# Output projections 2 and 3 as one Strassen product of 1024 tokens with operands scaled first; both groups' norms in the FFN

## The chip, the cores and the metric

The kernel runs on one core of one Trainium2 chip. The metric is device time in microseconds (us) of one execution; the number given for a kernel is the median of its runs.

## What is computed

One layer of a decoder trunk, 2048 tokens, width 1024, all in float32. Two groups of heads (a gated recurrence, "hgrn", and stick-breaking attention) each give 512 columns, which are normed per row, joined and sent through one output projection. A feed-forward network and a gated embedding follow. The part that the change touches:

```
o_hg = rmsnorm(hgrn2_mix(hq, hf, hi, lb), hg_out_norm) * silu(hg)
o_sb = rmsnorm(stick_breaking_mix(sq, sk, sv), sb_out_norm)
mix = concat([o_hg, o_sb], -1) @ w_out          # (2048, 1024) @ (1024, 1024)
h = h + rmsnorm(mix, attn_post_norm)
u = rmsnorm(h, ffn_pre_norm)
gate, up = split(u @ w_gate_up)
```

## The kernel before

Tokens are in four groups of 512 (`GT`), and the width is cut into 8 slices of 128 (`ND`; `HH` = 4 is half of it). A product in float32 is three matmuls: each operand is split into a rounded high part (a copy on ScalarE, ACT) and a low part (a subtraction on VectorE, DVE, or on GpSimd, POOL), and `mm3` (L214) adds hi x hi, hi x lo and lo x hi in one PSUM bank.

Stages follow each other: the input projection of the four groups with attention and hgrn woven in; output projections 0 to 3; gate/up, down and the embedding for two token pairs of 1024 each. The attention and hgrn outputs go to DRAM as `o_s[g][0..7]`, transposed, slices 0 to 3 from hgrn and 4 to 7 from attention.

An output projection (`out_proj(g)`, L640) takes the eight slices as operands (`out_load`, L618) and goes through four column quarters of the weights, two halves of the sum each (hgrn, attention), each with matmuls 256 columns wide: 384 a group. The norm of an input row is one factor per token, so it is put on after the matmul: ACT empties the hgrn half with the row's scale (L678), DVE adds the attention half with its own (L680). `post_mix(g)` (L693) norms `mix` (DVE L704), adds `x` (L705, DVE for one half and POOL for the other), norms again (ACT L709) and stores the rows to `un_s[g]` (L710). `turn` (L730) loads them (L737), transposes them on TensorE (L753), four per slice, applies the gain and stores `u_s[g]` (L759). Group 3 is different: its norms run late, in gate/up (`post_late`, L713), from rows stored to `h2_s`.

Gate/up, down and the embedding use Strassen's seven products over 1024 tokens: with both operands as 2 x 2 blocks, seven block products instead of eight, in the order `CHAIN` = 1, 2, 6, 3, 7, 5, 4 (L901), whose sums are chained: `chain` (L929) adds each product from PSUM to a running sum on DVE (L826 is that addition). Their weights' sums are made beforehand (`combos`), their token operands by `t_first` (L863, products 1, 2, 6) and `t_second` (L872, the rest).

The order of TensorE's work is written by hand: `weave(main, slots, ...)` (L51) takes two steps of `main` per slot and between them a share of steps of the other streams. The other engines' instructions are put in order by a scheduler; each engine and SyncE (SP), which issues the DMAs, then runs its own list strictly in order. Around the change the loop was: `post_mix(0)` and `turn(un_s[0])` beside output projection 1; `post_mix(1)` beside projection 2 and 3, `turn(un_s[1])` beside projection 3, together with the operands of gate/up's first three products (`first_operands`, `third_operands`); in gate/up, by hooks at its steps, `t_second`, `post_late(3)`, `turn` of groups 2 and 3.

## Time and profile before

| | us |
|---|---|
| median of 3 runs | 2997.5 |
| least and most of them | 2997.17, 2997.6 |
| the profiled execution's own time | 2997.89 |
| its span | 2995.8 |
| output projections 2 and 3, first to last of their time on TensorE | 1328.5 to 1456.5 |

The profiled execution is the source of all durations. Its engines are PE (TensorE), DVE (VectorE), ACT (ScalarE), POOL (GpSimd) and SP (SyncE). A group's row names the line, the engine, the operation, `out<-in` and its shape, then busy time, mean ns of one, and the idle time of the engine just before with what ended it. A row of waits reads: waiting instruction, releaser, total us, count, longest.

### The profile page before, as it was taken

The numbers are of one execution on the slowest core, as the hardware profiler recorded it, in microseconds if no ns is written. First come the engines' busy times: TensorE is split into PE (matmuls) and PEld (weight loads), VectorE is DVE, ScalarE is ACT, GpSimd is POOL, SyncE is SP. The second block draws the span as 40 slices with busy tenths as digits, with TensorE's granted clock in tenths as the row PEclk, the third lists the DMA queues.
The fourth block names the chain that finished last, engine by engine and source line by source line (L and its number), as shares of the span: only waits on it lengthen the run. The fifth ranks groups of instructions, "written<-read, shape, count | busy, mean of one in ns | idle before, by whom it ended". The sixth has DMA issues, their size and how long they took to land. (4 is left out here: it accounts for less than half of the span.)

```text
span 2995.8 us, 52519 instructions
## 1 busy us (share of the span) xinstructions
PE 2897.3 (97%) x18188; PEld 2425.5 (81%) x18188; DVE 2061.5 (69%) x2993; ACT 1581.0 (53%) x3182; POOL 1405.1 (47%) x1396
## 2 busy tenths in 40 slices
PE   8899999999999999897899999999999999999999
PEld 7788888888887888787788888788788888878777
DVE  3566667687777776755887687665777765656685
ACT  5666756676767676756533333455433323545542
POOL 3344555555556666754532222355622121456653
PEclk9999999999999999999999999999999999999999
DMA  7675665465445544567866787776965555677974
GB/s 215 205 214 166 184 177 165 146 179 166 150 142 152 151 145 128 163 201 244 281 201 197 245 289 253 249 206 213 339 203 163 166 176 176 207 219 230 328 249 162
DMA packets 469417, 602.26 MB, mean 201 GB/s; under 512 B 43168, under 2 KB 277664, under 8 KB 469152
## 3 DMA queue, kind: packets, MB, share of 16 engines
q1 hardware_dynamic: 469152, 598.91, 63.4%
q8 instruction: 144, 2.36, 0.3%
q14 instruction: 121, 0.99, 0.1%
HBM read 439.89 MB, written 158.86 MB: 200 GB/s over the span
## 5 line engine op out<-in xcount | busy, mean ns | idle before, releaser
L818 ACT CAST wh<-wr 128x512 fp32r<-128x512 f32 x600 | 351.6, 618 | 491.7 <-PE z L216 126.5
L819 POOL TENSOR_TENSOR wl<-wr,wh 128x512 fp32r<-128x512 f32 x256 | 371.1, 1456 | 466.2 <-ACT wh L818 426.8
L441 POOL TENSOR_TENSOR a<-be,ring 128x512 f32<-128x512 f32 (+2 forms) x320 | 320.4, 1002 | 411.6 <-DVE ring L437 372.8
L819 DVE TENSOR_TENSOR wl<-wr,wh 128x512 fp32r<-128x512 f32 x344 | 305.2, 895 | 177.5 <-ACT wh L818 160.0
L215 PE MATMUL mm<-uh,wh 128*128 128x512 f32 x992 | 411.3, 415 | 8.1 <-DVE vv L356 3.5
L217 PE MATMUL mm<-uh,wl 128*128 128x512 f32 x992 | 390.8, 394 | 0.0
L216 PE MATMUL mm<-ul,wh 128*128 128x512 f32 x992 | 389.5, 393 | 0.0
L437 DVE TENSOR_TENSOR_SCAN ring<-z,ring,be 128x512 f32<-128x512 f32 x192 | 245.7, 1280 | 101.9 <-ACT z L423 97.3
L215 PE MATMUL mm<-wh,uh 128*128 128x256 f32 (+1 forms) x936 | 287.3, 307 | 4.9 <-DVE vv L356 4.8
L216 PE MATMUL mm<-wl,uh 128*128 128x256 f32 (+1 forms) x936 | 273.5, 292 | 1.1 <-POOL wl L202 1.0
L217 PE MATMUL mm<-wh,ul 128*128 128x256 f32 (+1 forms) x936 | 273.1, 292 | 0.0
L201 ACT CAST wh<-wr 128x512 fp32r<-128x512 f32 x288 | 178.3, 620 | 130.7 <-PE mm L216 69.6
L202 POOL TENSOR_TENSOR wl<-wr,wh 128x512 fp32r<-128x512 f32 x144 | 190.0, 1320 | 103.7 <-ACT wh L201 91.7
L422 ACT ACTIVATE be<-z 128x512 f32<-128x512 f32 (+2 forms) x320 | 171.1, 535 | 106.5 <-DVE z L420 67.8
L215 PEld LDWEIGHTS mm<-uh,wh 128*128 128x128 f32 x992 | 187.6, 189 | 46.8 <-DVE eb L342 3.8
L454 DVE TENSOR_TENSOR al<-tr,ah 128x512 fp32r<-128x512 f32 (+1 forms) x320 | 191.5, 599 | 47.8 <-ACT ah L452 45.8
L217 PEld LDWEIGHTS mm<-uh,wl 128*128 128x128 f32 x992 | 186.9, 188 | 43.2
L819 POOL TENSOR_TENSOR wl<-s,wh 128x512 fp32r<-128x512 f32 x44 | 75.3, 1713 | 305.6 <-ACT wh L818 285.1
L216 PEld LDWEIGHTS mm<-ul,wh 128*128 128x128 f32 x992 | 187.9, 189 | 32.6
L452 ACT CAST ah<-tr 128x512 fp32r<-128x512 f32 (+1 forms) x320 | 167.8, 524 | 79.8 <-PE tr L449 74.6
L215 PEld LDWEIGHTS mm<-wh,uh 128*128 128x128 f32 x936 | 179.7, 192 | 13.4 <-issue 2.6
L416 PE MATMUL z<-kt,q 128*128 128x512 f32 (+3 forms) x640 | 187.8, 375 | 0.0
(312 smaller groups left out, 7559.9 us busy)
## 6 DMA issues: line engine op xcount, KB each, us to landing
wr<-in_w_gate_up_dram SPq DMA_DIRECT2D x308, 256.0 KB, 3.9
wr<-in_w_in_dram SPq DMA_DIRECT2D x224, 256.0 KB, 3.1
wr<-hid_s SPq DMA_DIRECT2D x154, 256.0 KB, 3.3
wr<-in_w_down_dram SPq DMA_DIRECT2D x110, 256.0 KB, 3.5
wr<-wd_s SPq DMA_DIRECT2D x88, 256.0 KB, 3.0
kt<-k_s SPq DMA_DIRECT2D x80, 256.0 KB, 3.3
vt<-v_s SPq DMA_DIRECT2D x80, 256.0 KB, 3.2
wr<-h_s SPq DMA_DIRECT2D x80, 256.0 KB, 4.2
```

The lines of the kernel that those rows point to most:

```text
L201: nc.scalar.copy(hi, src)
L202: (lo_engine or nc.gpsimd).tensor_tensor(lo, src, hi.bitcast(F32), op=ALU.subtract)
L215: nc.tensor.matmul(o, l[0], r[0], start=start, stop=False)
L216: nc.tensor.matmul(o, l[0], r[1], start=False, stop=False)
L217: nc.tensor.matmul(o, l[1], r[0], start=False, stop=stop)
L416: nc.tensor.matmul(z[:, :n], st["q"][i][:, tb * P:(tb + 1) * P], ch["k"][:, :n], start=i == 0, stop=i == 1)
L422: nc.scalar.activation(be[:, :n], z[:, :n], AF.Sigmoid, scale=0.125)
L437: nc.vector.tensor_tensor_scan(r[:, o:o + n][:, ::-1], z[:, :n][:, ::-1], be[:, :n][:, ::-1], init, op0=ALU.mult, op1=ALU.bypass)
L441: nc.gpsimd.tensor_tensor(a[:, :n], be[:, :n], r[:, o + 1:o + n + 1], op=ALU.mult)
L454: nc.vector.tensor_tensor(lo[:, lo_c:], tr[:, lo_c:], hi[:, lo_c:].bitcast(F32), op=ALU.subtract)
L818: nc.scalar.copy(hi, src)
L819: lo_engine.tensor_tensor(lo, src, hi.bitcast(F32), op=ALU.subtract)
```

## The change

Output projections 2 and 3 become one product of 1024 tokens, `out_pair(2)`. Its left operand is [group 2; group 3] x [hgrn half, attention half], its right one is `w_out` in four blocks; the seven products each take four row tiles x four slices x three matmuls of 512 columns.

Since Strassen adds blocks of the operands, the row factors can't be put on afterwards. So the operands are scaled first: `over_rows` turns a row factor into a tile that has it along every partition (a broadcast transposed on PE, copied by ACT), `scaled` multiplies (and applies the attention gain) and stores to `on_s`. For group 2 this is `first_rows(2)`, beside output projection 1, where group 3's squares of slices 4 to 6 are summed too. Group 3's own slices are loaded at the head of `out_pair`, and their scales are made at steps (0,1), (0,3) and (1,1) of it (product's place in the chain, row tile).

The sums of the weight blocks are made by `out_combos` in the first input projection (16 loads, 16 DVE subtractions, 16 stores to `wo_s`). `post_mix(1)`, `turn(un_s[1])` and `first_operands` are woven into `out_pair`; product 6's operands of gate/up move into gate/up's hooks, where its first two blocks now run products 1, 2 of each before 6 of each. The norms of group 2 are done late, as group 3's were (`post_late(2)`). Attention's rest is spread over 30 slots instead of 32.

Three places of the order. First SP, around the last attention tile's store (`avo` to `o_s[3][7]`). Before:

```order
L605 DMA o_s_3_140<-gate 128x512
L623 DMA raw<-o_s_3_140 128x512
L623 DMA raw<-o_s_4_141 128x512
L623 DMA raw<-o_s_5_142 128x512
L623 DMA raw<-o_s_6_143 128x512
L759 DMA u_s_99<-ev 128x512
L210 DMA wr<-in_w_out_dram 128x2x256
L472 DMA o_s_7_144<-avo 64x512
L210 DMA wr<-in_w_out_dram 128x2x256
L623 DMA raw<-o_s_7_144 128x512
```

And in the changed kernel, where L964 is a load to a `wr` tile and L474 the same store:

```order
L920 DMA u_s_99<-ev 128x512
L866 DMA h_s_88<-h 128x512
L474 DMA o_s_7_152<-avo 64x512
L866 DMA h_s_88<-h 128x512
L964 DMA wr<-o_s_0_145 128x512
L964 DMA wr<-o_s_1_146 128x512
L964 DMA wr<-o_s_2_147 128x512
L964 DMA wr<-o_s_3_148 128x512
L964 DMA wr<-o_s_4_149 128x512
L964 DMA wr<-o_s_5_150 128x512
L964 DMA wr<-o_s_6_151 128x512
L964 DMA wr<-o_s_7_152 128x512
```

All eight loads of group 3 stand behind that store, where four stood ahead of it and one behind. Second PE, around the first transposes of `un_s[1]`. Before, in output projection 3:

```order
L215 MATMUL z<-wh,uh 128x256
L216 MATMUL z<-wl,uh 128x256
L217 MATMUL z<-wh,ul 128x256
L753 MATMUL tr<-ident,xt 128x128 x4
L215 MATMUL mm<-wh,uh 128x256
L216 MATMUL mm<-wl,uh 128x256
L217 MATMUL mm<-wh,ul 128x256
```

Now, where the matmuls on bank `z` are the last of product 3's second row tile, those on `av` the first of its third, and L914 is the transposes:

```order
L217 MATMUL z<-wh,uh 128x512
L218 MATMUL z<-wl,uh 128x512
L219 MATMUL z<-wh,ul 128x512
L914 MATMUL tr<-ident,wr 128x128 x4
L217 MATMUL av<-wh,uh 128x512
L218 MATMUL av<-wl,uh 128x512
L219 MATMUL av<-wh,ul 128x512
```

The transposes have moved to between these two row tiles. Third DVE, around the last two row tiles of `post_mix(1)` (the L704 that reads `rstd`). Before:

```order
L704 SCALAR_TENSOR_TENSOR mix<-mix,rstd_18309,gb 128x512 x2
L819 TENSOR_TENSOR ul<-wr,uh 128x512
L705 TENSOR_TENSOR h<-h,mix 128x512
L202 TENSOR_TENSOR wl<-wr,wh 128x512
L819 TENSOR_TENSOR ul<-wr,uh 128x512 x4
L680 SCALAR_TENSOR_TENSOR mix<-z,rg,mix 128x256
L704 SCALAR_TENSOR_TENSOR mix<-mix,rstd_18403,gb 128x512 x2
L819 TENSOR_TENSOR wl<-wr,wh 128x512
L705 TENSOR_TENSOR h<-h,mix 128x512
```

Now L864 and L865 are those lines, L987 reading a bank is the chain addition, L204, L774 and L980 are splits; `c_18794`, `c_18839` and `c_18900` belong to product 3's row tiles 0, 1 and 2:

```order
L987 TENSOR_TENSOR c_18794<-mm,cu 128x512
L204 TENSOR_TENSOR ul<-wr,uh 128x512
L774 TENSOR_TENSOR ul<-wr,uh 128x512
L987 TENSOR_TENSOR c_18839<-z,cu 128x512
L204 TENSOR_TENSOR ul<-wr,uh 128x512
L864 SCALAR_TENSOR_TENSOR mix<-mix,rstd_18626,gb 128x512 x2
L865 TENSOR_TENSOR h<-h,mix 128x512
L864 SCALAR_TENSOR_TENSOR mix<-mix,rstd_18734,gb 128x512 x2
L865 TENSOR_TENSOR h<-h,mix 128x512
L980 TENSOR_TENSOR ul<-wr,uh 128x512 x2
L987 TENSOR_TENSOR c_18900<-av,cu 128x512
```

Both row tiles' norms now stand behind the chain addition of product 3's second row tile. The diff, without buffers' and pools' declarations:

```diff
+    def out_combos():
+        for k in range(HH):
+            ts = [xt("wo") for _ in range(4)]
+            for n, t in enumerate(ts):
+                r = (HH * (n // 2) + k) * P
+                nc.sync.dma_start(t, w_out[r:r + P, n % 2 * GT:(n % 2 + 1) * GT])
+            b_combos(*ts, V)
+            for i, t in zip((1, 3, 4, 2), ts):
+                nc.sync.dma_start(wo_s[k][i - 1], t)
+            yield
+
+    def square_sums(acc, first, g, ks, new):
+        for k in ks:
+            raw = new()
+            nc.sync.dma_start(raw, o_s[g][HH + k])
+            if k == first:
+                nc.scalar.activation(acc, raw, AF.Square)
+            else:
+                nc.scalar.activation(raw, raw, AF.Square)
+                nc.gpsimd.tensor_tensor(acc, acc, raw, op=ALU.add)
+
+    def tile_sums(acc):
+        b = bank("tr")
+        for t in range(TT):
+            nc.tensor.matmul(b[:, t:t + 1], acc[:, t * P:(t + 1) * P], ones1, start=True, stop=True)
+        ss = const.tile([P, TT], F32, tag="rq", name="rq", bufs=2)
+        nc.vector.tensor_copy(ss, b[:, 0:TT])
+        return ss
+
+    def row_scale(rr):
+        nc.gpsimd.tensor_scalar(rr, rr, 1.0 / (HH * P), EPS, op0=ALU.mult, op1=ALU.add)
+        nc.gpsimd.tensor_tensor(rr, rr, neghalf.to_broadcast((P, TT)), op=ALU.pow)
+        return rr
+
+    def over_rows(rr, tag, new):
+        b = bank(tag)
+        for t in range(TT):
+            nc.tensor.transpose(b[:, t * P:(t + 1) * P], rr[:, t:t + 1].to_broadcast((P, P)), ident)
+        e = new()
+        nc.scalar.copy(e, b)
+        return e
+
+    def scaled(g, i, raw, r):
+        if i < HH:
+            (nc.gpsimd if g == NG - 1 else nc.vector).tensor_tensor(raw, raw, r, op=ALU.mult)
+        else:
+            nc.vector.scalar_tensor_tensor(raw, raw, g_sb[:, i - HH:i - HH + 1], r, op0=ALU.mult, op1=ALU.mult)
+        nc.sync.dma_start(on_s[g][i], raw)
+
+    def first_rows(g, tt):
+        acc = ev(name="oss")
+        square_sums(acc, 0, g, range(HH), xt)
+        yield
+        ss = tile_sums(acc)
+        rr = row_scale(hgss[:, g, :]), row_scale(ss)
+        yield
+        for part in range(2):
+            r = over_rows(rr[part], "tr", xt)
+            yield
+            for k in range(HH):
+                raw = xt("raw")
+                nc.sync.dma_start(raw, o_s[g][part * HH + k])
+                scaled(g, part * HH + k, raw, r)
+                tt[1 + part, k] = split(wpool, "u", UB, raw, V if k % 2 else G)
+                if k % 2:
+                    yield
+
+    def out_pair(g, tt, acc):
+        sw = {}
+        cs = [{} for _ in range(TT)]
+        raws, s2 = {}, {}
+
+        def w_prep(pos, k):
+            prod = CHAIN[pos]
+            raw = wpool.tile([P, GT], F32, tag="wr", name="wr", bufs=4)
+            if prod in (1, 2, 3):
+                i, j = {1: (0, 0), 2: (1, 0), 3: (1, 1)}[prod]
+                r = (HH * i + k) * P
+                nc.sync.dma_start(raw, w_out[r:r + P, j * GT:(j + 1) * GT])
+            else:
+                nc.sync.dma_start(raw, wo_s[k][{5: 1, 6: 2, 7: 3, 4: 4}[prod] - 1])
+            if pos % 2:
+                hi, lo = slot("wh", 0, "wh", F32R), slot("wl", 0, "wl", F32R)
+            else:
+                hi, lo = operand(wpool, "u", UB)
+            nc.scalar.copy(hi, raw)
+            (V if k % 2 else G).tensor_tensor(lo, raw, hi.bitcast(F32), op=ALU.subtract)
+            sw[prod, k] = hi, lo
+
+        def a_prep(pos, k):
+            prod = CHAIN[pos]
+            if prod == 3:
+                a12 = load(on_s[g][HH + k])
+                sub(V, s2[k], a12, s2[k])
+                t, e = s2[k], G
+            elif prod == 7:
+                t, a21 = load(on_s[g][k]), load(on_s[g + 1][k])
+                sub(V, t, t, a21)
+                e = V
+            elif prod == 5:
+                t, a22 = load(on_s[g + 1][k]), load(on_s[g + 1][HH + k])
+                add(V, t, t, a22)
+                e = G
+            else:
+                t, e = load(on_s[g + 1][HH + k]), V
+            tt[prod, k] = split(wpool, "u", UB, t, e)
+
+        def rows(half, j, i):
+            m = cs[i][1 + half, 1 + j]
+            nc.sync.dma_start(h2_s[g + half][i * P:(i + 1) * P, j * GT:(j + 1) * GT], m)
+            nc.scalar.activation(junk, m, AF.Square, scale=ROOT, accum_out=sums_m[half][:, 2 * i + j:2 * i + j + 1])
+
+        def before(pos, i):
+            if (pos, i) == (0, 1):
+                raws["r"] = [over_rows(row_scale(hgss[:, g + 1, :]), "tr", new_acc)]
+                for k in range(HH):
+                    scaled(g + 1, k, raws[k], raws["r"][0])
+            elif (pos, i) == (0, 3):
+                raws["ss"] = row_scale(tile_sums(acc))
+            elif (pos, i) == (1, 1):
+                raws["r"].append(over_rows(raws["ss"], "tr", new_acc))
+                for k in range(HH):
+                    scaled(g + 1, HH + k, raws[HH + k], raws["r"][1])
+                    t = load(on_s[g][k])
+                    sub(V, t, raws[k], t)
+                    add(V, t, t, raws[HH + k])
+                    s2[k] = t
+                    tt[6, k] = split(wpool, "u", UB, t, G if k % 2 else V)
+
+        def new_acc():
+            return slot("acc", 0, "acc")
+
+        for pos in range(2):
+            for k in range(HH):
+                w_prep(pos, k)
+        for k in (*range(HH), *range(HH, ND)):
+            raws[k] = load(o_s[g + 1][k])
+        sq = new_acc()
+        nc.scalar.activation(sq, raws[ND - 1], AF.Square)
+        nc.gpsimd.tensor_tensor(acc, acc, sq, op=ALU.add)
+        for pos, prod in enumerate(CHAIN):
+            for i in range(TT):
+                before(pos, i)
+                b = mm_bank()
+                for k in range(HH):
+                    mm3(b, cut(tt[prod, k], i), sw[prod, k], k == 0, k == HH - 1)
+                chain(prod, cs[i], b, new_dn)
+                if prod == 2:
+                    rows(0, 0, i)
+                elif prod == 5:
+                    rows(0, 1, i)
+                    rows(1, 1, i)
+                elif prod == 4:
+                    rows(1, 0, i)
+                if 1 <= pos < len(CHAIN) - 1 and i < 2:
+                    for k in (2 * i, 2 * i + 1):
+                        w_prep(pos + 1, k)
+                        if pos > 1:
+                            a_prep(pos + 1, k)
+                yield
+            if prod in (5, 4):
+                half = 0 if prod == 5 else 1
+                for t in range(TT):
+                    row_rstd(None, rows_m[half][t], sums_m[half][:, 2 * t:2 * t + 2])
...
+        n = g - (NG - 2)
         for t in range(TT):
...
         if grp == 0:
-            for part in (CHAIN[:3], CHAIN[3:]):
+            for part in (CHAIN[:2], CHAIN[2:3], CHAIN[3:]):
                 for b in blocks[:2]:
                     steps += [b[p] for p in part]
...
-        weave(main, slots - tail, ra.part(slots - tail), rh.part(slots - tail, 1 if hg_n < slots else None))
+        more = ((Stream(out_combos()), HH, 1),) if n == 0 else ()
+        weave(main, slots - tail, ra.part(slots - tail), rh.part(slots - tail, 1 if hg_n < slots else None), *more)
...
-    rates = Rate(att_stream, 2, todo, 2 * OP_SLOTS)
+    rates = Rate(att_stream, 2, todo, 2 * OP_SLOTS - 2)
...
-    for g in range(NG - 1):
-        if g + 1 < NG - 1:
-            out_load(g + 1, res[g + 1])
+    tto = {}
+    for g in range(2):
         op = Stream(out_proj(g, res[g]))
         if g == 0:
+            out_load(1, res[1])
             weave(op, 2, rates.part(2), r2.part(2))
             hgs[2].drain()
             weave(op, OP_SLOTS - 2, rates.part(OP_SLOTS - 2), r3.part(OP_SLOTS - 2))
-        elif g == 1:
-            weave(op, half, rates.part(half), r3.part(half), (pm, TT, 0))
+        else:
+            rows = Stream(first_rows(2, tto))
+            weave(op, half, rates.part(half), r3.part(half), (pm, TT, 0), (rows, 3, 1))
             tu = Stream(turn(un_s[0], u_s[0], g_ffn, ["tr"], xt, ev))
-            weave(op, half, rates.part(half), r3.part(half), (tu, 9, 0))
+            acc3 = ev(name="oss")
+            square_sums(acc3, 0, 3, range(HH - 1), xt)
+            weave(op, half, rates.part(half), r3.part(half), (tu, 9, 0), (rows, 6, 1))
             hgs[3].drain()
             att_stream.drain()
+            rows.drain()
             side.close()
             big[0] = ctx.enter_context(tc.tile_pool(name="bigr", bufs=1, side="right"))
             mm_tags[:] = ["mm", "z", "mm", "z", "av"]
-        else:
-            out_load(NG - 1, res[NG - 1])
-            weave(op, half, (pm, TT, 0))
-            weave(op, half, (Stream(first_operands()), ND, 1))
         op.drain()
         pm = Stream(post_mix(g, res[g]["mix"]))
 
     drive = Drive([(gate_up(0, tt0), 3), (down(0), 4), (gate_up(1, tt1), 3), (down(1), 4),
                    (ple(0, ss0), 5), (ple(1, ss1), 5)])
+    op = Stream(out_pair(2, tto, acc3))
+    tu = Stream(turn(un_s[1], u_s[1], g_ffn, ["tr", "hg"], lambda: slot("wr", 0, "wr"), ev))
+
+    weave(op, 2)
+    weave(op, 5, (pm, TT, 0))
+    weave(op, 5, (tu, 9, 0), (Stream(first_operands()), ND, 1))
     drive.prepare(2)
-    op = Stream(out_proj(NG - 1, res[NG - 1]))
-    tu = Stream(turn(un_s[1], u_s[1], g_ffn, ["tr", "hg"], xt, ev))
-    weave(op, half + 2, (pm, TT, 0), (tu, 9, 0))
-
-    def third_operands():
-        for k in range(ND // 2):
-            t_first(0, tt0, 6, k)
-            yield
-
-    weave(op, half - 2, (Stream(third_operands()), ND // 2, 0))
...
 
     for k in range(ND // 2):
-        at(0, k, lambda k=k: t_second(0, tt0, k))
-    spread(0, 17, post_late(NG - 1), 2 * TT, 4)
+        at(0, k // 2, lambda k=k: t_first(0, tt0, 6, k))
+        at(0, 2 + k // 2, lambda k=k: t_second(0, tt0, k))
+    spread(0, 6, post_late(NG - 2), 2 * TT, 3)
+    spread(0, 19, post_late(NG - 1), 2 * TT, 4)
     for k in range(DFF // 256):
         at(0, 36 + 4 * k, lambda k=k: down_combos(k))
-    spread(0, 36, turner(un_s[2], u_s[2], g_ffn), 9, 2)
-    spread(0, 54, turner(h_s[3], u_s[3], g_ffn, rows_h), 9, 2)
+    spread(0, 36, turner(h_s[2], u_s[2], g_ffn, rows_h[0]), 9, 2)
+    spread(0, 54, turner(h_s[3], u_s[3], g_ffn, rows_h[1]), 9, 2)
```

More of the change, by code (lines that the diff above doesn't have):

```diff
@@ L123, in hybrid_block @@
     hid_s = [dram.tile([DFF // 256, 7, P, GT], F32, tag=f"hid_s{i}", name=f"hid_s{i}") for i in range(2)]
+    on_s = scratch("on_s", (ND, P, GT))
+    wo_s = [dram.tile([4, P, GT], F32, tag=f"wo_s{k}", name=f"wo_s{k}") for k in range(ND // 2)]
     o_s = [[dram.tile([P, GT], F32, tag=f"o_s{g}_{i}", name=f"o_s{g}_{i}") for i in range(ND)] for g in range(NG)]
@@ L271, in row_rstd @@
         return out
-    row_scales = ctile("row_scales", (P, 4 * TT))
-    rows_m, rows_h = ([row_scales[:, i * TT + t:i * TT + t + 1] for t in range(TT)] for i in range(2))
-    sums_m = row_scales[:, 2 * TT:4 * TT]
+    row_scales = ctile("row_scales", (P, 2, 4 * TT))
+    rows_m, rows_h = ([[row_scales[:, n, i * TT + t:i * TT + t + 1] for t in range(TT)] for n in range(2)] for i in range(2))
+    sums_m = [row_scales[:, n, 2 * TT:4 * TT] for n in range(2)]
     UB = 16
@@ L682, in out_proj @@
                     yield
-                if g == NG - 1 and o == 1 and part == 1:
-                    for t in range(TT):
-                        m = mix[t][half]
-                        nc.sync.dma_start(h2_s[g][t * P:(t + 1) * P, half * GT:(half + 1) * GT], m)
-                        nc.scalar.activation(junk, m, AF.Square, scale=ROOT, accum_out=sums_m[:, 2 * t + half:2 * t + half + 1])
-        res["mix"] = mix
-        if g == NG - 1:
-            for t in range(TT):
-                row_rstd(None, rows_m[t], sums_m[:, 2 * t:2 * t + 2])
+        res["mix"] = mix
@@ L721, in post_late @@
                 gb = load(attn_post_norm[0:1][:, cs].to_broadcast((P, GT)))
-                nc.vector.scalar_tensor_tensor(m, m, rows_m[t], gb, op0=ALU.mult, op1=ALU.mult)
+                nc.vector.scalar_tensor_tensor(m, m, rows_m[n][t], gb, op0=ALU.mult, op1=ALU.mult)
                 nc.gpsimd.tensor_tensor(h, h, m, op=ALU.add)
@@ L726, in post_late @@
                 if j == 1:
-                    row_rstd(None, rows_h[t], ss)
+                    row_rstd(None, rows_h[n][t], ss)
                 yield
```

## The prediction

> **What bounds the kernel now.** I read the page first, for the engine that is busiest over the whole span.
>
> ```profile
> span 2995.8 us, 52519 instructions
> PE 2897.3 (97%) x18188; PEld 2425.5 (81%) x18188; DVE 2061.5 (69%) x2993; ACT 1581.0 (53%) x3182; POOL 1405.1 (47%) x1396
> ```
>
> TensorE (PE) has work in 2897.3 of 2995.8 us, so what can be had is PE work removed or one of the few stretches in which it idles. The change replaces the stage of output projections 2 and 3, so next I cut the span by stage. The view of windows gives, per window, its length, the busy time and count of PE, weight loads, DVE, ACT and POOL, then the granted PE clock, the DMA share and GB/s.
>
> ```profile
> 140.00:270.00 130.00, 127.03 (x733) 108.76 (x732) 86.91 (x149) 83.84 (x181) 58.85 (x64) 1.00 0.66 195
> 1280.00:1328.50 48.50, 47.86 (x558) 44.23 (x558) 24.65 (x42) 27.77 (x56) 24.70 (x29) 0.99 0.56 179
> 1328.50:1456.50 128.00, 104.73 (x818) 102.13 (x818) 71.91 (x104) 82.19 (x184) 63.34 (x65) 0.93 0.82 282
> 1420.00:1430.00 10.00, 9.65 (x81) 9.33 (x79) 4.55 (x10) 8.88 (x20) 6.08 (x7) 1.00 1.06 384
> 1456.50:1500.00 43.50, 38.46 (x161) 30.77 (x160) 41.70 (x52) 22.11 (x41) 29.96 (x21) 0.96 0.63 208
> ```
>
> The third row is the stage: 128.0 us, a fifth of it PE idle, and the clock down to 0.93. Its neighbours matter because the change puts work there: the second half of output projection 1 (second row) has PE full and DVE half free; the start of gate/up (last row) has DVE full; the early input projection (first row) is PE-bound with room elsewhere. The PE waits of the stage (wait, releaser: total us, count, longest) say who ends them:
>
> ```profile
> PE z L215 <- ACT mix L678: 11.3, 1, 11.3
> PE z L216 <- POOL wl L202: 3.7, 3, 1.5
> PE z L215 <- ACT wh L201: 3.6, 2, 1.9
> PE av L216 <- POOL wl L202: 1.7, 2, 1.0
> PE av L215 <- ACT wh L201: 1.4, 1, 1.4
> PE mm L216 <- POOL wl L202: 1.0, 1, 1.0
> ```
>
> These six rows are 22.7 us: one wait of 11.3 for a bank that ACT had to empty, the rest for weights not yet split. The timeline gives the rate of the matmuls, as the distance between two starts, 256 wide here and 512 wide in gate/up:
>
> ```profile
> 1351.10 0.28 PE L217 MATMUL mm<-wh,ul 128*128 128x256 f32 x1
> 1351.22 0.28 PE L215 MATMUL mm<-wh,uh 128*128 128x256 f32 x1
> ...
> 1555.11 0.40 PE L216 MATMUL mm<-ul,wh 128*128 128x512 f32 x1
> 1555.34 0.39 PE L217 MATMUL mm<-uh,wl 128*128 128x512 f32 x1
> ```
>
> So 0.12 us for 256 columns, 0.23 for 512. The stage's 768 matmuls are 768 x 0.12 = 92.2 us; 128.0 - 92.2 - 22.7 leaves 13.1 us for transposes, the small sum matmuls and matmuls slowed by the clock.
>
> **The matmuls.** The change has 7 products x 4 tiles x 4 k x 3 = 336 matmuls of 512 columns: 336 x 0.23 = 77.3 us, 14.9 less. The six waits above belong to code that is gone, so -22.7 as well. The 13.1 us I keep: the same 32 transposes stay, 12 small matmuls come for 16, and the clock's share I work out behind the waits. Without new waits the stage would thus be 77.3 + 13.1 = 90.4 us. What comes back are four waits. I call the stage's head E (1328.5 before) and use a tile's pace 12 x 0.23 = 2.76 us.
>
> **Three early waits.** Group 3's eight raw loads now stand on SP behind the store of the last attention tile, and the sum of squares needs the eighth load.
>
> ```profile
> 1331.75 0.60 SPq L472 DMA_DIRECT2D o_s<-avo  x1
> ...
> DMA to landing us min/median/max: 2.7/2.7/2.7
> L634 ACT ACTIVATE raw<-raw 128x512 f32<-128x512 f32 x3 | 1.9, 622 | 0.6 <-DVE ul L628 0.6
> L635 POOL TENSOR_TENSOR oss<-oss,raw 128x512 f32<-128x512 f32 x3 | 3.9, 1292 | 2.7 <-ACT raw L634 2.6
> L202 POOL TENSOR_TENSOR wl<-wr,wh 128x512 fp32r<-128x512 f32 x16 | 23.1, 1447 | 32.2 <-ACT wh L201 30.0 <-DMA wr<-in_w_out_dram 1.3 <-DMA gb<-in_attn_post_norm_dram 0.8
> L651 POOL TENSOR_SCALAR rg<-rg 128x8 f32<-128x8 f32 x2 | 0.9, 434 | 1.7 <-DVE rg L650 1.7
> L652 POOL TENSOR_TENSOR rg<-rg,neghalf 128x8 f32<-128x8 f32 x2 | 3.7, 1840 | 0.2
> L628 DVE SCALAR_TENSOR_TENSOR ul<-raw,g_sb,uh 128x512 fp32r<-128x512 f32 x4 | 3.0, 741 | 4.3 <-ACT uh L627 4.3
> L819 DVE TENSOR_TENSOR ul<-wr,uh 128x512 fp32r<-128x512 f32 x20 | 17.3, 879 | 7.0 <-ACT uh L818 6.9
> L826 DVE TENSOR_TENSOR c<-z,cu 128x512 f32<-128x512 f32 x6 | 4.1, 679 | 0.0
> L823 DVE TENSOR_TENSOR wr<-wr 128x512 f32<-128x512 f32 x28 | 23.3, 856 | 2.3 <-DMA wr<-u_s 1.9 <-DMA wr<-in_w_gate_up_dram 0.3
> ```
>
> The first wait: the store was issued at E+3.3 and landed 2.7 us later, E+6.0. Eight loads of 262 KB at the 384 GB/s of the 1420 window take 5.5: E+11.5. Square 0.62, add 1.29: E+13.4. PE, after three tiles (8.3) and a few transposes, is there at E+8.7: it waits about 4.8.
>
> The second: the row scale of that half must be transposed before the second product's second tile. In POOL's order four multiplies by the row scale and one split (no such multiply before; the split's 1.45 each) and then 0.43 + 1.84 stand in between: 5 x 1.45 + 2.27 = 9.5, so E+22.9. PE, freed at 13.4, has two tiles to do, 5.5, and small work: E+19.4. Wait 3.5.
>
> The third: product 6's operands. From E+22.9 a copy (0.62), then on DVE four scalings like L628 (3.0), eight subtractions and additions of 0.86 (6.8), three chain additions of 0.68 (2.0) and three splits of 0.88 (2.6): E+37.9; PE, with three more tiles (8.3), arrives at E+31.6 or a little later: 6 at most, and since one split is POOL's and some chain additions fall behind, I take 4. The sum is 12.3; from 6, if the loads overlap the store, to 16.
>
> **The fourth wait: transposes of group 1.** In the order that I showed, post_mix(1) of the last two row tiles stands on DVE behind the chain addition of product 3's second tile, and the transposes stand on PE right behind that tile. All four row tiles must be normed, stored to un_s and loaded back in between, and PE has nothing else. Before, the same sequence ran beside projection 3 with 12 us of other matmuls ahead of the transposes; its length can be read:
>
> ```profile
> 1364.03 1.41 DVE L704 SCALAR_TENSOR_TENSOR mix<-mix,rstd,gb 128x512 f32<-128x512 f32 x2 [0.20 <-POOL rstd L270]
> 1384.57 0.42 SPq L737 DMA_DIRECT2D xt<-un_s  x1
> DMA to landing us min/median/max: 2.1/2.9/4.7
> L705 DVE TENSOR_TENSOR h<-h,mix 128x512 f32<-128x512 f32 x8 | 10.6, 1328 | 1.3 <-PE z L217 0.8 <-DMA h<-in_x_dram 0.4
> L705 POOL TENSOR_TENSOR h<-h,mix 128x512 f32<-128x512 f32 x8 | 12.5, 1558 | 4.0 <-PE tr L753 2.1 <-DVE mix L704 1.3 <-DMA h<-in_x_dram 0.6
> ```
>
> The norm of row tile 2 began at 1364.03, the load of un_s was issued at 1384.57 and landed 2.9 later: 23.4 us. With the chain addition ahead (0.68) that is 24 us of PE gap. The lower end: between the two pairs of L704 six other DVE operations stood, now none; 6 x 0.88 = 5.3 less, 19. The upper: three weight splits on POOL (1.45 each) fall between: 28. I take 24, since the row is the same work.
>
> **The clock after the waits.** A clock of 0.93 on 104.7 busy us is 7 of the 13.1 us. One window holds the return from the 11.3 us wait, which ended at 1363.4:
>
> ```profile
> 1360.00:1370.00 10.00, 6.64 (x45) 6.64 (x46) 7.00 (x9) 6.15 (x15) 6.59 (x6) 0.69 0.35 130
> ```
>
> There 6.64 busy us ran at 0.69: 2 us lost by one wait. Four waits at 2 are 8, against 7 now; so the 13.1 stay. The Trainium skill, "TensorE: Matmul & The Clock Gate", Part 1, has the clock halved by an idle window of about 3.4 us and restored after as long a busy one, an estimate of 1.7 us for each long wait. By it one long wait now and four later, the sum would be 5 us higher; the 2 us of the window agree with its size, but the stage loses 7 with one long wait, so short waits count too, and the row decides.
>
> **Stage.** 90.4 + 12.3 + 24 = 126.7 against 128.0: -1.3. The low ends give 90.4 + 6 + 19 = 115, the high ends 90.4 + 16 + 28 = 134.
>
> **Beside the stage.** Group 2's scaling moves into the second half of output projection 1. DVE gets 13 operations more, 13 x 0.86 = 11 us on 24.65 of 48.5 busy, and POOL some; SP gets 16 loads and 8 stores. There is room, but they stand in order among steps that PE waits for: +1 (0 to 6). The weight combinations (16 subtractions, 13.7 us, and 32 transfers, 8.4 MB) go where DVE is busy 86.9 of 130 and DMA moves 195 GB/s: hidden, +0.5 (0 to 3). If the cover failed, the 13.7 us would come due. In gate/up, product 6's operands (4 x about 2.7 us of DVE) come later, where DVE has 41.7 of 43.5 busy and this row:
>
> ```profile
> PE tr L217 <- DVE wl L819: 5.0, 2, 2.7
> ```
>
> But the first two products of both blocks run first, 2 x 2 x 2 x 2.76 = 22 us and more of cover: 0 (-5 to +8). Group 2's late norm there needs nothing from PE: 0 while PE is the bound. Together +1.5; stage and rest -1.3 + 1.5 = +0.2. The profiled execution of before took 2997.89 us by its own clock around the span of 2995.8; the median is 2997.5, 0.4 off. 2997.9 + 0.2 = 2998.1.
>
> **Rivals.** The first: faster. What speaks for it are the -37.6 us of matmuls and old waits, which are sure, while the new waits are bounds of mine. With the early waits at 6 (-6.3), the gap at 19 (-5) and no price beside the stage (-1.5): 2998.1 - 12.8 = 2985. Against it: the fourth wait follows from the order, and only its length is open. Chance 0.34.
>
> The second: slower, because DVE becomes the bound of the stage. It has some 97 operations there: 27 chain additions at 0.68 (18.4), 24 sums and differences at 0.86 (20.6), 33 splits at 0.88 (29.0), 10 scalings and norms (8.5), 3 residual additions at 1.33 (4.0), together 81 us. All but the chain additions, 70, read two operands from SBUF, and POOL runs some 30 operations beside them. The rows above show the spread: the chain addition, one operand from PSUM, takes 679 ns, L705 on DVE 1328 with POOL's own L705 beside it. If each POOL operation holds one of them up by 1.0 (between 1.33 - 0.68 and POOL's own 1.45), 81 becomes 111; with the 24 us in which the norms' chain passes through ACT, POOL and DMA and DVE mostly waits, 135, so +7 on the stage and +1.5 beside: 2997.9 + 8.5 = 3006. It decides when these 70 take 128 - 24 - 18.4 = 85.6 us, 1.22 each instead of 62/70 = 0.89. Chance 0.17. The Trainium skill, "SBUF — State Buffer", section "Who interferes with whom", says that the two engines lock each other out of a shared port for a whole instruction; the difference between 679 and 1328 agrees; if each of the 30 cost its full length, the time would be some 13 us more.
>
> The third: slower, because transfers bound it.
>
> ```profile
> DMA packets 25801, 36.15 MB, mean 282 GB/s; under 512 B 2198, under 2 KB 14230, under 8 KB 25789
> ```
>
> By the order 39.1 MB are moved from the head of the stage to gate/up's first weights. At 384 GB/s that is 102 us, hidden; at this stage's mean of 282, 139 us, +11 and +1.5: 3010. After the gap 75 transfers (19.7 MB) queue up, of which 9.2 MB are needed within 33 us: 24 us at 384, 33 at 282. So it decides near 280 GB/s. The 1420 window speaks against. Chance 0.12.
>
> That the change doesn't do what it says I leave at nothing: the removed matmuls are gone from the order.
>
> **How the numbers follow.** A measurement of this kernel tells some 0.2%, 6 us, from no change. Forecast, within that: 0.37, at 2998.1, its own range 2992 to 3004. Faster 0.34, slower 0.17 + 0.12 = 0.29. The range takes the first rival with stage and price at their lower ends, 2998.1 - 18, and the third with a little of the second: 2980 to 3012, which leaves out 2 in 10.
>
> **What would show it.** Right: a PE gap of 19 to 28 us ahead of the transposes behind product 3's second tile, ended by a load of un_s; waits of about 5, 3.5 and 4 at the sum matmuls, the second scale's transposes and product 6; a stage of about 127 us. The third rival shows in DMA at a share near 1 and waits for wo_s and on_s in the last three products; the second in DVE without idle time and two-SBUF additions past 1.2 us. Wrong would be a gap under 12 us, which says that the last norms ran ahead of that tile, or PE waits in output projection 1 or the input projection of more than a few us.

## The result and the profile after

The changed kernel takes 3024.2 us (median of 5 runs, 3015.6 to 3028.3) against 2997.5: ratio 1.008, 95% interval 1.0067 to 1.0094. It is slower by some 0.8%, above the predicted range. The profiled execution is the fastest of the five, 3015.62 us. Its page:

```profile
span 3013.8 us, 51897 instructions
PE 2869.5 (95%) x17772; PEld 2401.6 (80%) x17772; DVE 2105.5 (70%) x3035; ACT 1575.3 (52%) x3174; POOL 1425.1 (47%) x1412
```

PE has 28 us less work, as meant, and the span is 18 us longer. The windows show where PE idles: second half of output projection 1, the new stage, the head of gate/up, gate/up to where the late transposes end.

```profile
1271.00:1341.00 70.00, 54.24 (x584) 49.94 (x584) 41.34 (x65) 36.92 (x75) 38.04 (x42) 0.90 0.66 213
1341.00:1464.60 123.60, 90.96 (x385) 73.15 (x385) 80.94 (x100) 64.90 (x137) 65.98 (x61) 0.85 0.84 285
1464.60:1533.40 68.80, 52.24 (x210) 41.11 (x209) 55.59 (x76) 28.26 (x53) 32.15 (x22) 0.88 0.73 241
1533.40:1953.90 420.50, 402.68 (x1765) 329.18 (x1764) 315.38 (x458) 147.74 (x286) 110.46 (x82) 0.98 0.75 247
```

The new stage, the second row, takes 123.6 us where the old one took 128. It was outside of it that time was lost. To put numbers on that, I cut each trace at the same matmuls of the three-line helper `mm3`, counted from the start up to the new stage and from the end behind it; the stretches below are the differences of their start times, in us. The cuts are the start of projection 0, the end of projection 1, the first matmul of gate/up, and the matmuls with 6200, 4500 and 1 left.

| kernel | to projection 0 | projections 0, 1 | stage | head of gate/up | gate/up on | rest |
|---|---|---|---|---|---|---|
| before | 1100.0 | 210.8 | 128.2 | 54.9 | 404.9 | 1073.9 |
| after | 1103.2 | 219.4 | 123.8 | 68.8 | 420.5 | 1054.5 |
| difference | +3.2 | +8.6 | -4.4 | +13.9 | +15.6 | -19.4 |

With 0.6 from the start these give 18.1, the difference of the last matmuls. The last stretch gains 19.4 us with nothing changed in it.

**The stage.** PE's waits in it, in the changed kernel:

```profile
PE tr L914 <- DMA wr<-un_s: 21.8, 2, 13.8
PE tr L712 <- POOL oss L827: 5.4, 1, 5.4
PE z L218 <- POOL ul L774: 3.1, 1, 3.1
PE z L218 <- DVE ul L774: 1.9, 1, 1.9
```

And the chain of the first row, on DVE, SP and PE:

```profile
1401.28 0.68 DVE L987 TENSOR_TENSOR c<-z,cu 128x512 f32<-128x512 f32 x1
...
1403.40 1.42 DVE L864 SCALAR_TENSOR_TENSOR mix<-mix,rstd,gb 128x512 f32<-128x512 f32 x2 [0.84 <-POOL rstd L272]
...
1409.91 1.42 DVE L864 SCALAR_TENSOR_TENSOR mix<-mix,rstd,gb 128x512 f32<-128x512 f32 x2 [4.49 <-POOL rstd L272]
```

```profile
1415.62 0.93 SPq L870 DMA_DIRECT2D un_s<-mix  x2
1417.74 1.40 SPq L898 DMA_DIRECT2D wr<-un_s  x3
```

```profile
1406.29 0.66 PE L914 MATMUL tr<-ident,wr 128*128 128x128 f32 x2 [7.95 <-DMA wr<-un_s]
1420.77 0.69 PE L914 MATMUL tr<-ident,wr 128*128 128x128 f32 x2 [13.82 <-DMA wr<-un_s]
```

Row tile 2's norm follows the chain addition of product 3's second row tile, row tile 3's follows that, then store, load and the transposes: the predicted fourth wait, in two pieces.

**The losses.** The 3.2 us before projection 0 are taken up with the weights' sums below. In projections 0 and 1 PE waited 27.4 us in all, 19.8 before; the largest rows, before and after:

```profile
PE hg L595 <- DVE sl L591: 7.0, 4, 2.9
PE hg L531 <- DVE ks L570: 3.6, 3, 2.4
PE hg L531 <- DVE gate L604: 2.6, 1, 2.6
PE tr L449 <- POOL a L441: 2.4, 1, 2.4
```

```profile
PE tr L914 <- DMA xt<-un_s: 8.3, 1, 8.3
PE hg L597 <- DVE sl L593: 6.5, 4, 2.9
PE hg L544 <- DVE ks L572: 4.1, 3, 3.1
PE hg L533 <- POOL qp L570: 3.6, 4, 1.8
```

The wait for the load of `un_s[0]` in projection 1 is new and makes up the difference; waits for hgrn's vector steps (bank `hg`) stood there before too. At the head of gate/up PE waits for splits, and in gate/up, at the late transposes, for ScalarE's copies, where 0.2 us were waited before (the last row):

```profile
PE mm L219 <- DVE wl L980: 6.1, 1, 6.1
PE mm L218 <- POOL ul L980: 5.0, 1, 5.0
PE mm L217 <- ACT uh L979: 4.2, 1, 4.2
...
PE hg L914 <- ACT acc L919: 11.6, 4, 3.7
```

```profile
PE hg L753 <- ACT acc L758: 0.2, 1, 0.2
```

DVE at the head, in the window that holds those waits, has no room: 34.31 of 35 us.

```profile
1480.00:1515.00 35.00, 22.68 (x87) 16.78 (x86) 34.31 (x48) 15.67 (x29) 16.10 (x8) 0.87 0.56 174
```

**The gain.** A full window of gate/up, before and after; the number to read is the count of PE instructions in 100 us at a clock of 1.00.

```profile
2280.00:2380.00 100.00, 100.00 (x436) 81.65 (x435) 73.88 (x109) 30.01 (x50) 17.52 (x13) 1.00 0.55 173
```

```profile
2280.00:2380.00 100.00, 100.00 (x443) 82.84 (x442) 72.30 (x104) 30.13 (x51) 21.84 (x16) 1.00 0.55 173
```

100/436 is 0.2294 us, 100/443 is 0.2257: the same matmuls follow each other 1.6% faster. Over the 1074 us at the end that is 17 of the 19.4 us.

### The profile page after: what moved, and what is told of

It reads as the page before. It is cut to its first block, busy times and chain, and to the rows that moved or that the text cites. A ratio compares the mean times of both kernels' runs of the same rounds, so it can differ in the third digit from the quotient of the medians.

```text
span 3013.8 us, 51897 instructions
## 1 busy us (share of the span) xinstructions
PE 2869.5 (95%) x17772; PEld 2401.6 (80%) x17772; DVE 2105.5 (70%) x3035; ACT 1575.3 (52%) x3174; POOL 1425.1 (47%) x1412
## 5 line engine op out<-in xcount | busy, mean ns | idle before, releaser
L980 POOL TENSOR_TENSOR wl<-wr,wh 128x512 fp32r<-128x512 f32 x256 | 375.2, 1473 | 437.4 <-ACT wh L979 390.3
L979 ACT CAST wh<-wr 128x512 fp32r<-128x512 f32 x600 | 350.7, 618 | 437.5 <-PE mm L218 91.2
L980 DVE TENSOR_TENSOR wl<-wr,wh 128x512 fp32r<-128x512 f32 x344 | 305.3, 895 | 179.2 <-ACT wh L979 154.5
L217 PE MATMUL mm<-wh,uh 128*128 128x256 f32 (+1 forms) x856 | 266.7, 312 | 4.2 <-DVE vv L358 4.2
L218 PE MATMUL mm<-wl,uh 128*128 128x256 f32 (+1 forms) x856 | 252.6, 295 | 2.6 <-POOL wl L980 2.6
L219 PE MATMUL mm<-wh,ul 128*128 128x256 f32 (+1 forms) x856 | 252.2, 295 | 0.0
L203 ACT CAST wh<-wr 128x512 fp32r<-128x512 f32 x256 | 158.7, 620 | 125.2 <-PE mm L218 65.2
L204 POOL TENSOR_TENSOR wl<-wr,wh 128x512 fp32r<-128x512 f32 x128 | 168.6, 1317 | 81.7 <-ACT wh L203 75.3
L980 POOL TENSOR_TENSOR wl<-s,wh 128x512 fp32r<-128x512 f32 x44 | 67.9, 1547 | 259.2 <-ACT wh L979 232.5
L451 PE MATMUL tr<-ident,a 128*128 128x128 f32 x1088 | 175.8, 275 | 8.3 <-POOL a L443 8.0
```

The costliest lines, as they stand in the source:

```text
L204: (lo_engine or nc.gpsimd).tensor_tensor(lo, src, hi.bitcast(F32), op=ALU.subtract)
L217: nc.tensor.matmul(o, l[0], r[0], start=start, stop=False)
L218: nc.tensor.matmul(o, l[0], r[1], start=False, stop=False)
L219: nc.tensor.matmul(o, l[1], r[0], start=False, stop=stop)
L451: nc.tensor.transpose(tr[:, tb * P:(tb + 1) * P], ch["a"][tb][:, sb * P:(sb + 1) * P], ident)
L979: nc.scalar.copy(hi, src)
```

## Experiments

**The pitch of the matmuls.** First the changed kernel unaltered.

> The changed kernel once more, unaltered. In its first profile the 512-wide matmuls from the new stage to the end start 0.227 us apart, against 0.231 before, which over the 6400 matmuls of gate/up and after is worth some 19 us, although the profiled run was the fastest of five (3015.6 of 3015.6 to 3028.3). Theory A: the pitch is an accident of the execution or the chip; then it differs here, and with 0.231 the time is about 3035. Theory B: the pitch belongs to the changed kernel (its tiles lie elsewhere); then it is 0.227 again and the time stays within 3015 to 3028, the spread having another cause. Under both the waits stand where they stood: 22 us ahead of the transposes in the new stage, 8 in output projection 1, 15 at the head of gate/up, 12 at the late transposes.

3024.1 us, ratio to before 1.0076 (1.0049 to 1.0103), profiled at 3026.6. The pitch is the same as in the first profile, and so are the waits, in place and within 1 us. The spread among the runs has another cause; most of it shows in projections 0 and 1, 225.7 us here and 219.4 in the first profile. PE waited there for the same 27 us in both, but the mean granted clock was 0.92 here and 0.95 in the first (windows 1121 to 1349 and 1121 to 1341). The stretches below are to be read with that in mind. Theory B, then. Of what both kernels have in common, two things lie elsewhere in SBUF: the tiles of the left pools behind `row_scales`, and those of the right pool, which are in another order. The first, tried on the kernel before:

```diff
-    row_scales = ctile("row_scales", (P, 4 * TT))
+    row_scales = ctile("row_scales", (P, 8 * TT))          # b_pad; 4 * TT + 24: b_pad96; 4 * TT + 32: b_pad128
```

> The kernel before with nothing but its row_scales tile made as large as the changed kernel's (64 bytes more per partition, unused), so that what is allocated behind it lies elsewhere. If the pitch of the 512-wide matmuls hangs on where the tiles lie at that small shift: 0.227 in gate/up and 2997.5 - 19 to 24 = about 2976. If not: 0.231 and 2997.5, within 0.1%.

> The kernel before with row_scales made 96 bytes larger per partition, unused: by the declarations this is what the changed kernel's small tiles add in all (64 for row_scales, 32 for rq). The shift of 64 left the pitch in gate/up at 0.231, though it fell to 0.229 to 0.230 in places. Theory A, the pitch goes with the exact address of the tiles: 0.227 here, and 2998 - 20 = 2978. Theory B, it goes with something else of the changed kernel (the pools' places or what the stage leaves behind): 0.231 and within 0.2% of before.

> The kernel before with row_scales made 128 bytes larger per partition, unused, so that the operand tiles of the left pools start at the very bytes where the changed kernel's do (45024 for the first, against 44896 before, 44960 and 44992 in the two runs with less padding). Theory A, the pitch of 0.227 goes with that address: 0.227 from gate/up on and about 2978. Theory B, it needs also the changed kernel's order of tiles in the right pool, or has nothing to do with addresses: 0.231 and within 0.2% of before.

> The same, and the right pool's tiles laid out in the changed kernel's order too (weights' parts first, then loads, sums, operands), by naming them once when the pool is opened. Every operand tile from gate/up on then lies where the changed kernel has it. Theory A, addresses make the pitch: 0.227 and about 2978. Theory B, something else does: 0.231 and within 0.2% of before.

Ratios to before: 0.9985 (0.997 to 1.0001), 1.0013 (1.0 to 1.0025), **0.9927 (0.9898 to 0.9956)** and 0.9936 (0.9914 to 0.9959), the last two at 2975.1 and 2979.5 us. The same window with 96 bytes of padding, then with 128:

```profile
2280.00:2380.00 100.00, 100.00 (x434) 81.17 (x433) 75.11 (x111) 30.96 (x52) 17.95 (x13) 1.00 0.54 171
```

```profile
2280.00:2380.00 100.00, 100.00 (x443) 82.84 (x442) 68.17 (x102) 30.95 (x52) 19.33 (x14) 1.00 0.50 154
```

64 and 96 bytes, each a guess at the right amount, leave the pitch as it was (437 and 434 in the window); with 128 bytes the first tile lies where the changed kernel has it, and the pitch is the changed kernel's. The last 32 bytes decide, with no instruction changed: 434 or 443. The order of the right pool's tiles (`b_ord128`) does nothing to the pitch, 443 again. Then the reverse, the changed kernel moved back by 64 bytes:

```diff
-        ss = const.tile([P, TT], F32, tag="rq", name="rq", bufs=2)
+        ss = const.tile([P, 2 * TT], F32, tag="rg", name="rg", bufs=2)[:, 0:TT]
```

> The changed kernel with the small sums' tile sharing the buffers of the row factors' tile, so that the operand tiles of the left pools start at byte 44960 instead of 45024, where the padded kernel before had its pitch of 0.231; nothing else differs. Theory A, the changed kernel owes its pitch to that address alone and its own price is hidden behind it: 0.231 from gate/up on, and 15 to 22 us slower than the unaltered changed kernel, about 3040. Theory B, the changed kernel has the pitch anyhow: 0.227 and 3020 to 3028.

3033.1 us, ratio 1.0126 (1.0101 to 1.0151). The window again:

```profile
2280.00:2380.00 100.00, 100.00 (x436) 81.66 (x435) 72.18 (x105) 30.82 (x52) 24.57 (x16) 1.00 0.55 174
```

The pitch is back, the last stretch is 1074.5 instead of 1054.5 to 1057.6. The total rose by 9, under the 15 expected; in the profiles its earlier stretches are together 11 us shorter than in the repeated run. So the changed kernel's own price is 1.26% where it has the old pitch, or 3024.2 - 2975.1 = 49 us against `b_pad128`, which has the new one; what was measured, 27, has an accidental gain in it. The profiles of the changed kernel and `b_pad128` differ by +4.7, +11.8, -6.4, +15.9, +16.5 and -0.5 us in the six stretches: with the same pitch in both, the last one is level.

**The weights' sums alone**, added to the kernel before and not used:

> The kernel before with out_combos alone added in the first input projection; its sums are stored and not used. Theory A, the 3.2 us that the changed kernel is later at the end of that stage are these 32 transfers and 16 subtractions: the matmul that stood at 401.2 stands 3 to 4 us later here, and all that follows too, about 3001. Theory B, they come from elsewhere (the clock, the start): less than 1 us.

2994.7 us in one run. To projection 0 it takes 1102.8 us; the five kernels before without the sums take 1098.5 to 1103.1, mean 1099.9, the profiles of the changed kernel 1103.2 to 1105.6. A cost of 3 to 4 us fits, but one run inside that spread doesn't show it, and by the end of projection 1 it is gone (207.9 there).

**Output projection 1.** Three kernels: all nine steps of `first_rows` in the last half (`a_op1`), attention over 32 slots again (`a_rate32`), and `first_rows` without its squares, row factors, transposes and multiplications (`a_norows`, whose group 2 goes unscaled into the product).

```diff
-            weave(op, half, rates.part(half), r3.part(half), (pm, TT, 0), (rows, 3, 1))
+            weave(op, half, rates.part(half), r3.part(half), (pm, TT, 0))                       # a_op1
-            weave(op, half, rates.part(half), r3.part(half), (tu, 9, 0), (rows, 6, 1))
+            weave(op, half, rates.part(half), r3.part(half), (tu, 9, 0), (rows, 9, 1))          # a_op1
-    rates = Rate(att_stream, 2, todo, 2 * OP_SLOTS - 2)
+    rates = Rate(att_stream, 2, todo, 2 * OP_SLOTS)                                             # a_rate32
...
-                scaled(g, part * HH + k, raw, r)
+                nc.sync.dma_start(on_s[g][part * HH + k], raw)                                  # a_norows
```

> The changed kernel with all nine steps of first_rows(2) in the last half of output projection 1 instead of three in the one half and six in the other, so that post_mix(0) has the vector engine, ScalarE and GpSimd to itself as before. Theory A, the squares and sums of group 2 delay post_mix(0) and so un_s[0]: the 9 us of PE waiting for it fall to under 4, and the end of the projection comes 4 to 6 us earlier. Theory B, PE only gets there earlier because attention is spread over 30 slots: the wait stays above 7. Both expect that the operands of group 2 may be late at the head of the stage instead; that would be a new wait before the first product, up to 10 us.

> The changed kernel with attention spread over 32 slots again. Theory A, the second half of output projection 1 is longer because PE's hgrn and attention steps are packed in fewer slots and PE comes to the transposes of group 0 early: the 9 us of waiting for un_s fall to 5 or less and the projection's end stands 3 to 5 us earlier than in the unaltered changed kernel. Theory B, the work of first_rows on the other engines is the cause: wait and end within 2 us of the unaltered one (from output projection 0's start to 1's end 219 to 226 us, against 211 before).

> The changed kernel with first_rows(2) left to load, store and split group 2's slices: the squares, the row factors, their transposes and the eight multiplications are left out, so group 2 goes unscaled into the product. Theory B, that this work delays post_mix(0) and the hgrn steps in output projection 1: from projection 0's start to 1's end about 211 to 213 us instead of 219 to 226, and 8 to 12 us off the total. Theory A, that the packing of attention does it: 217 or more.

Projections 0 and 1 take 224.9, 215.5 and 208.5 us (unaltered 219.4 and 225.7; before 210.8); the last two kernels took 3009.6 and 3004.3 us in one run each. In `a_op1` the wait for `un_s` is gone, and these stand in its place:

```profile
PE hg L597 <- DVE sl L593: 7.0, 2, 4.9
PE tr L712 <- POOL oss L707: 6.0, 1, 6.0
PE hg L583 <- ACT q L579: 2.0, 1, 2.0
```

Total 3018.1, ratio 1.006 (1.0039 to 1.0081). All of PE's waits in both projections are 26.2 us, against 27.4 unaltered: the work has to be done, and whatever it stands in front of is late. So theory A is right there that the squares and sums delay `un_s[0]`, and wrong that the projection ends earlier without them in the first half. With attention over 32 slots the wait for `un_s` stays at 8.7, as theory B has it, but hgrn's waits shrink, all waits are 24.1 us, and the stretch is 4 to 10 us shorter, which theory B doesn't have. The last kernel below, `a_best`, has the same 32 slots and the same 24.1 us of waits, but takes 218.2, so the gain in the stretch is little more than the spread among runs. Without the work itself the whole loss is gone: 19.9 us of waits, 19.8 before. The cause is `first_rows`; the packing of attention added some 3 us of waits to it.

**The gap in the stage.**

```diff
-    weave(op, 2)
-    weave(op, 5, (pm, TT, 0))
+    weave(op, 1)
+    weave(op, 4, (pm, TT, 0))
+    weave(op, 4)
     weave(op, 5, (tu, 9, 0), (Stream(first_operands()), ND, 1))
```

> The changed kernel with post_mix(1) woven into steps 2 to 9 instead of 4 to 13 and the transposes of group 1 from step 18 on instead of 14, so that four row tiles of matmuls (11 us) lie between. Theory A, that the gap is the length of the chain norm, store, load that nothing covers: the 21.8 us of waiting for un_s fall to under 8 and the time by about 14 to 20. Theory B, that the freed time meets the vector engine: gate/up's first operands are then late by as much and the head of gate/up waits longer, so that the time falls by under 8.

3015.9 us, ratio 1.0052 (1.0038 to 1.0066). Its longest wait:

```profile
PE tr L914 <- DMA wr<-un_s: 8.6, 1, 8.6
```

From 21.8 to 8.6, just short of theory A's mark of 8; the stage is 116.0 instead of 123.8 us, and the time falls by 8. Of the 13 us the time keeps 8: other waits in the stage grow (all of them from 32.7 to 22.7). The head of gate/up is 70.6 us instead of 68.8 and 69.6, so theory B, by which the head takes what the stage gains, doesn't hold.

**The head of gate/up.** Product 6's operands go back into the stage, gate/up's first blocks and `t_second` to their old order (parts of the edit):

```diff
-            for part in (CHAIN[:2], CHAIN[2:3], CHAIN[3:]):
+            for part in (CHAIN[:3], CHAIN[3:]):
...
+    weave(op, 2, (Stream(third_operands()), ND // 2, 0))
```

> The changed kernel with product 6's operands of gate/up prepared in the last four steps of the new stage again, and gate/up's first two blocks in the old order (1, 2, 6 of each). Theory A, that 12 vector operations more at the head of gate/up are what PE waits for there: the waits between 1490 and 1520 (16 us) shrink to about 5, and the time falls by 10 to 14. Theory B, that the vector engine is full from the new stage on and only hands the work around: the operations delay the last products of the new stage instead, and the time stays within 4 us.

3016.3 us, ratio 1.0049 (1.0032 to 1.0067): some 8 less, of which the head shows 4 (65.1 us), other stretches varying as between repeats. The waits there moved:

```profile
PE z L219 <- DVE wl L980: 3.3, 1, 3.3
PE tr L217 <- ACT wh L979: 3.1, 1, 3.1
PE z L217 <- ACT wh L979: 3.1, 1, 3.1
PE tr L218 <- DVE ul L980: 1.0, 1, 1.0
```

11.5 instead of 16, not 5: less than theory A expects. The test of both theories is all three remedies together.

> The changed kernel with the three remedies together: attention over 32 slots, post_mix(1) earlier and the transposes of group 1 later, and product 6's operands in the stage with gate/up's old order. Theory A, each wait was paid by itself: 5 for the rate, 8 to 14 for the transposes, 4 to 8 for the operands, in all 3024 - 17 to 27, so 2997 to 3007. Theory B, the vector engine hands the work around: the stage's end comes earlier, but the head of gate/up waits longer than 15 us, and the total stays above 3010. Both leave it well above the 2975 of the kernel before with the same addresses.

3008.8 us, ratio 1.0038 (1.0024 to 1.0051): 15 us less than unaltered, between the marks of the two theories (2997 to 3007, and above 3010). The single remedies' gains (8, 8, and for attention's slots 14 in one run, 4 to 10 by its stretch) come to more than that. The stage takes 118.0, and the head 69.5, as long as ever:

```profile
PE tr L217 <- ACT wh L979: 7.6, 1, 7.6
PE z L217 <- ACT wh L979: 4.3, 1, 4.3
PE z L219 <- DVE wl L980: 4.2, 2, 2.1
```

These waits are 16.1 us. In the head theory B fits: DVE, busy for 59.3 of 65 us in the window from 1460, hands its backlog on. Taking 12 operations off DVE there gained 4 us in `a_third`; where the rest of the head's 14 comes from is argued from its rows, not shown by a run.

**The late transposes**, first with the last norm stored in `post_late` instead of put on by `turn`, then with group 2's turn at step 30 instead of 36.

```diff
...
+                        nc.scalar.activation(m, h, AF.Copy, scale=r)
+                        nc.sync.dma_start(un_s[g][rows, cs], m)                   # a_un
...
-    spread(0, 36, turner(h_s[2], u_s[2], g_ffn, rows_h[0]), 9, 2)
+    spread(0, 30, turner(h_s[2], u_s[2], g_ffn, rows_h[0]), 9, 2)                 # a_eturn
```

> The changed kernel with the last norm of groups 2 and 3 put on in post_late, which stores the normed rows, so that turn has no scaling on ScalarE ahead of its copies (16 stores more, 24 small ACT operations fewer). Theory A, PE waits at the late transposes because ACT, in order, stands at a scaling whose load is late: the four waits (11 us) go and the time falls by 8 to 12. Theory B, the loads are late because SP stands behind the stores of the down combinations, and the stores added make that worse: the waits stay, ended by the load instead of ACT, and the time changes by less than 4.

> The changed kernel with the late turn of group 2 six steps earlier, at step 30 instead of 36 of gate/up, ahead of the down combinations. Theory A, its loads are late because SP stands behind the stores of those combinations: the two waits of PE for ScalarE's copies in group 2's transposes (7 to 8 us of the four) go, and gate/up from its 200th to its 1900th matmul is 6 to 9 us shorter. Theory B, the scaling ahead of the copies is late in any case: the waits stay within 2 us of before.

What is behind these waits is seen in the changed kernel's ACT, SP and PE:

```profile
1726.69 0.91 ACT L901 ACTIVATE wr<-wr,row_scales 128x256 f32<-128x256 f32 x2 [16.74 <-DMA wr<-h_s]
...
1729.34 0.67 ACT L919 ACTIVATE acc<-hg,g_ffn 128x512 f32<-128x512 f32 x1
```

```profile
1717.73 1.86 SPq L964 DMA_DIRECT2D wr<-in_w_gate_up_dram  x3
1723.73 0.97 SPq L898 DMA_DIRECT2D wr<-h_s  x2
```

```profile
1730.06 0.66 PE L914 MATMUL hg<-ident,wr 128*128 128x128 f32 x4 [3.74 <-ACT acc L919]
```

ACT stands 16.7 us at a scaling whose load SP issued late, and the copy that frees PE's bank is behind it. Taking the scaling away (`a_un`) leaves two waits with 9.1 us and 3017.4 us, ratio 1.0061 (1.0042 to 1.0081): two of the four waits go, but little of their sum, so the scaling isn't the cause alone. The time falls by 7, between theory B's 4 and theory A's 8 to 12. The earlier turn (`a_eturn`) leaves 7.6 us, the stretch 413.4 instead of 420, and 3018.7 in one run. By transposes, the waits in group 2's fall from 6.8 to 1.1 us, as theory A expects, and those in group 3's, which stand where they stood, go from 4.8 to 6.5. So for group 2 the load is late, and ACT passes it on. The time in the stretch is no proof: kernels with nothing changed there take from 413.7 (`a_turn2`) to 422.8 us (`a_best`). What the rest of that stretch's loss is stays open.

## Why the prediction was wrong

- **The matmuls, the stage and two of its four waits** were right: 123.8 us against 126.7 forecast (before 128). The gap is 21.8 for 24 and the wait for the sum of squares 5.4 for 4.8, by the chains that were forecast. In place of product 6's operands (4) PE waited 5.0 for splits of weights. The wait at the second row factor (3.5) didn't come: the factor was there at 1364.7, 23.7 us behind the stage's head for 22.9 forecast, but PE, whose matmuls started up to 0.43 us apart there, needed 8 us for the two tiles ahead of it, not 5.5, and came at 1365.1.
- **The clock** was misread, without harm to the sum. The 7 us before were worked out from a window's mean clock, which counts idle time too. By the trace's records of the granted clock, which stand at 1.0 and 0.5 only, PE's busy time lost an estimated 4.5 us in the stage before and 8.1 now. So keeping the 13.1 left out some 3.6 us, nearer to the 5 that the prediction set aside; the shorter waits (32.7 for 36.3) made up for it, which is luck.
- **The step that failed is "Together +1.5" for what lies beside the stage.** Measured: +3.2 before projection 0 (not clear of the spread), +8.6 in projections 0 and 1, +13.9 at the head of gate/up and +15.6 in the rest of it, 41 in place of 1.5. PE waits in output projection 1, which the prediction named as a sign of being wrong, came. The price of projection 1 was over its bound of 6 in the first profile and far over it in the repeat (14.9). I counted DVE's free time there (24.65 of 48.5) instead of what stands behind the added operations: `a_norows`, which leaves out nine of the 13 on DVE and their companions on ACT, POOL and PE, has none of the loss. Head of gate/up: bound +8, cost 13.9 to 14.7, on an engine that the prediction's own row showed at 41.70 of 43.50; putting product 6's operands back alone gained 4 of them. "Group 2's late norm ... 0" has no run of its own: PE waits 11.6 us at the late transposes, 6.8 in group 2's and 4.8 in group 3's, for 0.2 before, and how much of the +15.6 the late norm made stays open.
- **The second rival** had the right engine at the wrong place. DVE did not bound the stage, with 80.9 of 123.6 us: the 13 subtractions of L984 there took 1.385 us on average, but all its operations other than chain additions 0.95, and 1.22 was what the rival needed. DVE was full only in the head behind it. The 135 us did not occur. The Trainium skill, "SBUF — State Buffer", section "Who interferes with whom", fits the slow subtractions; no run here shows what they cost the total.
- **The third rival** was wrong: 285 GB/s in the stage, and no wait on a weight's or operand's transfer.
- **Not seen at all**: 19 us of gain from where tiles lie. At the old pitch the miss would have been larger, as `a_off` shows.

## What to carry to other kernels

Work that is moved beside a full engine is not free because the engine that takes it is half idle: look for what stands behind each moved operation in its engine's order, and for loads that an in-order engine meets there. When times differ where nothing was changed, compare the matmuls' pitch in a full window before explaining anything; try a few bytes of padding on the kernel before, as part of the comparison. Here that alone gives the fastest version of all, 2975.1 us, ratio 0.9927 to before.

## What the runs showed of the hardware

The start-to-start distance of 512-wide matmuls depended on where the left pools' tiles, the operands among them, lie in SBUF. Its mean in the window from 2300 to 2400 us was 0.2305 us when the left pools' first operand tile stood at byte 44896 of the program's allocation, 0.2307 at 44960, 0.2310 at 44992, and 0.2267 at 45024. The changed kernel has 0.2267 at 45024 and 0.2307 at 44960 too. The granted clock was 1.00 throughout. The right pool starts at 135136 throughout, which is the same remainder by 2048 as 45024 (2016); whether that is the rule wasn't tried. The first stages didn't change: between 300 and 400 us it was 0.231 to 0.232 in all of these kernels.
